# Part of a weight split moved from VectorE to GpSimd, and the matmul order around a triangular solve rewritten, in a hybrid decoder layer

## The chip, the cores and the metric

The kernel runs on one core of a Trainium2 chip. The metric is the device time of one execution in microseconds (us). The kernel before took 1213.77 us, the median of three runs (1211.12 to 1214.0). Engines are named as the profile names them: PE is TensorE, PEld its weight loads, DVE is VectorE, ACT is ScalarE, POOL is GpSimd and SP is SyncE, which here only issues loads.

## The reference, cut to what matters

One layer of a decoder for 256 tokens of width 2048, in float32:

```python
h = rms_norm(x, attn_norm_g)
proj = h @ w_in                                  # 2048 -> 4448 columns
h_r, h_k, h_v, h_w, h_a, h_g = token_shift(...)  # RWKV-7 heads, 16 x 64
c_q, c_kv, k_pe = ...                            # latent attention, 512 + 512 + 64
y_rwkv = rwkv7_mixer(...)                        # a recurrence over the 256 tokens
y_mla = mla_mixer(...)                           # 8 heads, causal softmax over 256 keys
x = x + concat(y_rwkv, y_mla) @ w_out
x = x + conv_glu_ffn(rms_norm(x), ...)           # 2048 -> 2 x 5632 -> 2048
return rms_norm(x)
```

In the recurrence a state S of 64 by 64 per head is updated by `S = S*w + (S a) b + v k` for every token, and `S r` is read out. The result is compared in float32, so the matmuls can't simply be rounded to a shorter type.

## The kernel before, in words

**Weight pieces.** All weights come in pieces of 128 x 1024 float32 (512 KB). `piece` (line 125) loads one on SP's queue into `raw` (three buffers), lets ACT write a rounded copy `hi` (line 133, three buffers), and lets DVE write the rest, `lo = raw - hi` (line 134, three buffers). An input product (`prod_c`, line 170) is then, for a piece, 16 matmuls with `hi` (line 175, high and low part of the activations) and 8 with `lo` (line 178). One tile of 128 output columns of `w_in` takes two pieces, h = 0 and h = 1.

**Order of the layer.** First the tiles of the decay, the keys (1 to 8), the receptances (9 to 16) and the values (17 to 24), in `in_tile` (line 201). Then the latent tiles 27 to 34 (`latent_tile`, line 801; x = 0 for the query latent, x = 1 for the key/value latent, four tiles each), the products from the latents (`up_b`, `up_v`), the chunks of the recurrence, the attention heads, the output projection, and from about 475 us on the feed-forward part, which the change doesn't touch.

**The factor.** The recurrence is done in four chunks of 64 tokens, and each chunk needs the inverse of a triangular matrix. `solve` (line 582) makes it: the masked products go to DRAM and back into `Lp` (POOL queue, line 580), DVE scales `Lp` (line 590) and does 31 steps of two operations each (lines 594 and 596), each on the result of the one before, then a reordered copy `tp` (line 598); POOL's queue writes it to DRAM (line 604), reads it back as `T11` (line 608) and does the same for `TT` (lines 606 and 613). On PE, `solve_r` (line 639) needs `T11`, `solve_t` needs `TT`, and all chunks come after.

**What sets the order.** PE's order around the chunks is written out by hand (`manual_schedule`, line 978). The work that doesn't belong to the recurrence is cut into 30 *units*, which the generator `all_units` (line 926) hands out: units 1 to 8 are the half tiles of the query latent, 9 to 16 those of the key/value latent, 17 to 20 the first products from the latents (unit 18 with `latent_rs(1)` and `rope_q`, unit 20 with the broadcast of `rrB1`), 21 to 30 the rest. `unit(11)` issues eleven of them before `chunk_a(0)` and `solve_r`; nine more stand one by one between the parts `chunk_a`, `chunk_b`, `chunk_c` of the chunks, three between the parts of the factor, and the rest between the heads (`step`). All other engines and queues are ordered by a planner, which fills each engine in time order from its own cost estimates, with what is ready and stands first in the program; the order so made is fixed, and each engine works it off in order.

**Buffers that the change touches.** `chunk_a` to `chunk_c`, the heads and `gn_out` share three PSUM buffers named `ch` (line 97), and the products share three named `mm`. In `chunk_c` the new state of both halves (`pS`, then DVE lines 734 to 737) came first, and then the outputs of both halves (`py`, copied by ACT, line 744). In the last part, `gn_out(0)` (transposes `pyT`, line 791) came before `step(7)`, the last head.

Of the kernel before, what the change touches and what calls it, by code (L numbers as in the profile page):

```python
# [9 lines left out]
F32 = mybir.dt.float32  # L10
# [4 lines left out]
ALU = mybir.AluOpType  # L15
# [3 lines left out]
T = 256  # L19
# [35 lines left out]
def hybrid_layer(ctx: ExitStack, tc: tile.TileContext, a: dict, out: bass.AP):  # L55
    nc = tc.nc
    V, S, PE = nc.vector, nc.scalar, nc.tensor
# [39 lines left out]
    def ch(n="ch"):  # L97
        return ps.tile([P, 512], F32, tag="ch", name=nm(n), bufs=NCH)
# [23 lines left out]
    nc.scalar.dma_start(vec, a["vec"])  # L122


    def piece(src, dst=None):
        raw = sb.tile([P, 1024], F32, tag="raw", name=nm("raw"), bufs=NRAW)
        last_w[0] = nc.sync.dma_start(raw, src).ins
        if dst is None:
            hi = sb.tile([P, 1024], F32R, tag="hi", name=nm("hi"), bufs=NHI)
            lo = sb.tile([P, 1024], F32R, tag="lo", name=nm("lo"), bufs=NLO)  # L130
        else:
            hi, lo = (dst.rearrange("p k t -> p (k t)")[:, q * 1024:(q + 1) * 1024] for q in range(2))
        S.copy(hi, raw)  # L133
        last_lo[0] = V.tensor_tensor(lo, raw, hi.bitcast(F32), ALU.subtract).ins  # L134
        return hi, lo

    def xsplit(g):
# [10 lines left out]
    last_w, last_lo, last_x, last_sh = [None], [None], [None], [None]  # L148
# [21 lines left out]
    def prod_c(acc, pieces, act, kt0, n, first, last):  # L170
        hi, lo = pieces
        acc = acc[:, :T]
        for j in range(n):
            for s in range(2):
                PE.matmul(acc, hi[:, j * P:(j + 1) * P], act(kt0 + j)[:, s, :], start=first and j == 0 and s == 0,  # L175
                          stop=False, skip_group_check=True)
        for j in range(n):
            PE.matmul(acc, lo[:, j * P:(j + 1) * P], act(kt0 + j)[:, 0, :], start=False,  # L178
                      stop=last and j == n - 1, skip_group_check=True)
# [19 lines left out]
    x_hl = lambda k: xs_[k // 4][:, k % 4, :, :]  # L199

    def in_tile(i, pf=mm):
        acc = pf()
        for h in range(2):
            prod_c(acc, piece(a["win"][i, h]), x_hl, h * 8, 8, h == 0, h == 1)
        flush()
        return acc

# [196 lines left out]
    PC = con([P, 8, 4], "PC")  # L404
# [280 lines left out]
    def pairs(dst, hf, terms, first=True):  # L685
        for n, term in enumerate(terms):
            for a_ in range(4):
                p = hf * 4 + a_
                for h in range(2):
                    lhsT, rhs = term(p, a_, h)  # L690
                    PE.matmul(dst[HS[h], a_ * 64:(a_ + 1) * 64], lhsT, rhs,
                              start=first and n == 0 and a_ == 0, stop=True, skip_group_check=True)
# [28 lines left out]


    def chunk_c(c):
        for hf in range(2):
            if c < 3:
                pS = ch("pS")
                pairs(pS, hf, [lambda p, a_, h: (BKt[c][:, p, HS[h]], UV[c][:, p, HS[h]])])
                for h in range(2):
                    hs = HS[h]
                    sv = ST[hf][hs, :, hs]  # L730
                    pSv = pS[hs, 0:256].rearrange("p (a v) -> p a v", a=4)
                    pcb = PC[hs, hf * 4:hf * 4 + 4, c:c + 1].broadcast_to([64, 4, 64])
                    if c > 0:
                        V.tensor_tensor(sv, pSv, sv, ALU.add)
                        V.tensor_tensor(sv, sv, pcb, ALU.mult)
                    else:
                        V.tensor_tensor(sv, pSv, pcb, ALU.mult)
        for hf in range(2):
            if c == 0:
                py[hf] = ch("py")  # L740
            pairs(py[hf], hf, [lambda p, a_, h: (G1[c][hf][:, h * 4 + a_, 64:128], UV[c][:, p, HS[h]])], c == 0)
            for h in range(2):
                yv = yt[c // 2][HS[c % 2], hf * 512:(hf + 1) * 512].rearrange("p (a h v) -> p a h v", a=4, h=2)
                ylast[c] = S.copy(yv[:, :, h, :], py[hf][HS[h], 0:256].rearrange("p (a v) -> p a v", a=4)).ins

    def gn_vec(w):
        y = yt[w]
# [53 lines left out]
    def latent_tile(x, j, gname):  # L801
        if j == 0:
            cl.append([s4(F32R, "cl").rearrange("p (k s t) -> p k s t", k=2, s=2) for _ in range(2)])
            css[x] = t2("css")
        i, acc = 27 + x * 4 + j, mm()
        prod_c(acc, piece(a["win"][i, 0]), x_hl, 0, 8, True, False)
        yield
        prod_c(acc, piece(a["win"][i, 1]), x_hl, 8, 8, False, True)
        cr, ssum = t2("cr"), css[x]
        V.tensor_tensor(cr, acc[:, :T], rsB, ALU.mult)  # L810
        if j == 0:
            S.activation(ssum, cr, AF.Square)
        else:
            sq = t2("csq")
            S.activation(sq, cr, AF.Square)
            V.tensor_tensor(ssum, ssum, sq, ALU.add)
        h_, l_ = (cl[x][j // 2][:, j % 2, q, :] for q in range(2))
        S.activation(h_, cr, AF.Copy, scale=vv(gname, j))
        V.scalar_tensor_tensor(l_, cr, vv(gname, j), h_.bitcast(F32), ALU.mult, ALU.subtract)
        yield  # L820
# [23 lines left out]
    def up_b(src, i, x, dsts):  # L844
        pcs = piece(src[i])
        for j in range(2):
            acc = mm()
            prod_c(acc, (pcs[0][:, j * 512:(j + 1) * 512], pcs[1][:, j * 512:(j + 1) * 512]),
                   lambda k: cl[x][k // 2][:, k % 2, :, :], 0, 4, True, True)
            if x == 0:  # L850
                S.copy(dsts[j], acc[:, :T])
            else:
                V.tensor_tensor(dsts[j], acc[:, :T], rrB1, ALU.mult)

# [106 lines left out]
    def out_piece(half, c, i):  # L961
        if i == 0:
            oacc[c] = [mm(), ch() if (half, c) == (1, 1) else mm()]
        if half == 1 and i == 2:
            load_x1(c)
        prod_a(oacc[c], piece(a["wout"][half, c, i]), lambda k: y_hl(yhi, half, k),
               lambda k: y_hl(ylo, half, k), i * 2, 2, i == 0, i == 3)
        if i == 3:
            for tb in range(2):
                V.tensor_tensor(x1[c][:, tb, :], x1[c][:, tb, :], oacc[c][tb], ALU.add)  # L970
# [3 lines left out]
    def unit(n=1):  # L974
        for _ in range(n):
            next(units)

    with tc.manual_schedule(engines={mybir.EngineType.PE}):
        unit(11)
        chunk_a(0)  # L980
        solve_r()
        unit()
        solve_t()
        unit()
        chunk_b(0)
        unit()
        chunk_c(0)
        gn = gn_vec(0)
        for c in range(1, 4):
            unit()  # L990
            chunk_a(c)
            if c == 3:
                next(gn)
            unit()
            chunk_b(c)
            if c == 3:
                next(gn)
            unit()
            chunk_c(c)
        next(gn)  # L1000
        g2a = s4(n="g2a")
        g2b = s4(n="g2b")
        gnwb = [s4(n=n) for n in ("gnw", "gnb")]
        with tc.issue_after(ylast[1]):
            for t, n in zip(gnwb, ("gnw", "gnb")):
                nc.scalar.dma_start(t, a[n].broadcast_to([P, 1024]))
            nc.scalar.dma_start(g2a, a["g2"][0:P])
            nc.scalar.dma_start(g2b[64:96], a["g2"][P:160])
        def step(h):
            attend_t(h)  # L1010
            if h < 7:
                scores(h + 1)
            attend(h)
            next(gn, None)

        scores(0)
        unit()
        next(gn)
        unit()
        step(0)  # L1020
        unit()
        step(1)
        unit()
        step(2)
        unit()
        out_piece(1, 0, 0)
        step(3)
        unit(2)
        assert next(units, None) is None
        step(4)  # L1030
        next(gn)
        out_piece(1, 0, 1)
        step(5)
        assert next(gn, None) is None
        gn_gate(0)
        out_piece(1, 0, 2)
        step(6)
        out_piece(1, 1, 0)
        gn_out(0)
        step(7)  # L1040
        out_piece(1, 0, 3)
        for _ in gn_vec(1):
            pass
        for i in range(1, 4):
            out_piece(1, 1, i)
# [194 lines left out]
```

## Time and profile before

| what | before |
|---|---|
| median of three runs | 1213.77 us |
| the profiled execution: its time / its span | 1213.11 us / 1211.3 us |
| mean granted PE clock in it | 0.982 |
| PE busy in it | 1167.2 us, 96% |
| DVE, ACT, POOL busy in it | 818.0, 589.0, 65.4 us |
| products `lo` on DVE (line 134), count and mean | 376, 1225 ns |

All times of the profile count from the start of the span. A busy PE is a PE that has matmuls in its pipeline; where its granted clock falls, the same matmuls take longer and it is busy all the same. In the timeline, the bracket at the end of a row is the idle time of that engine before it and what ended it.

### The profile page before, as it was taken

How to read it: one execution, taken by the hardware profiler on the slowest of the kernel's cores; microseconds unless marked ns; L12 is line 12 of the kernel's file. 1: busy time of each engine (PE TensorE's matmuls, PEld its weight loads, DVE VectorE, ACT ScalarE, POOL GpSimd, SP SyncE). 2: the span in 40 equal slices, each digit the busy share in tenths (PEclk: the TensorE clock that was granted, in tenths of full speed). 3: DMA queues.
4: the chain of work that ended last, by engine and by line, in shares of the span. 5: the costliest groups of instructions: out<-in, count | busy, mean ns of one | idle time of the engine just before them, and what ended most of it. 6: DMA issues, size and time to landing. Idle time of an engine off the chain costs nothing.

```text
span 1211.3 us, 19591 instructions
## 1 busy us (share of the span) xinstructions
PE 1167.2 (96%) x7629; PEld 1029.9 (85%) x7629; DVE 818.0 (68%) x1339; ACT 589.0 (49%) x897; POOL 65.4 (5%) x192
## 2 busy tenths in 40 slices
PE   7999999699989999999999999999999999999996
PEld 7899999688876788888888888888888888888885
DVE  6798659748857666777777776444477777766563
ACT  6584346324444355555555554333455555554542
POOL 1600430110000001000000000000000000000000
PEclk9999999879999999999999999999999999999998
DMA  9544455523433455555555555555655555566662
GB/s 323 199 136 149 140 170 177 183 77 104 162 106 106 161 185 176 190 192 192 192 192 191 191 192 187 192 189 188 205 192 189 193 192 191 190 223 209 209 212 84
DMA packets 61485, 215.90 MB, mean 178 GB/s; under 512 B 7376, under 2 KB 8144, under 8 KB 61392
## 3 DMA queue, kind: packets, MB, share of 16 engines
q1 hardware_dynamic: 58544, 209.22, 52.4%
q0 software_dynamic: 2080, 3.38, 1.1%
q10 hardware_dynamic: 768, 2.05, 0.5%
q8 instruction: 60, 0.98, 0.3%
q14 instruction: 33, 0.27, 0.1%
HBM read 210.48 MB, written 3.41 MB: 177 GB/s over the span
## 4 chain that ended last, share of the span: by engine, by line
PE 68%; DVE 1%; issue 1%; ACT 0%; ACTq 0%
PE mm L163 27%; PE mm L166 13%; PE mm L195 9%; PE mm L196 9%; PE mm L197 9%; PE pxT L1068 0%; PE pgate L782 0%; PE pgate L783 0%; PE mm L175 0%; DVE lo L134 0%; PE po L920 0%; PE ch L196 0%; PE ch L195 0%; PE ch L197 0%; ACT pexp L898 0%
## 5 line engine op out<-in xcount | busy, mean ns | idle before, releaser
L134 DVE TENSOR_TENSOR lo<-raw,hi 128x1024 fp32r<-128x1024 f32 x376 | 460.4, 1225 | 293.3 <-ACT hi L133 284.3
L133 ACT CAST hi<-raw 128x1024 fp32r<-128x1024 f32 x376 | 395.1, 1051 | 503.3 <-PE mm L163 160.4
L163 PE MATMUL mm<-z,hi 128*128 128x512 f32 x1408 | 351.4, 392 | 0.0
L163 PEld LDWEIGHTS mm<-z,hi 128*128 128x128 f32 x1408 | 252.1, 188 | 43.4
L166 PEld LDWEIGHTS mm<-z,lo 128*128 128x128 f32 x1408 | 188.4, 188 | 14.3
L166 PE MATMUL mm<-z,lo 128*128 128x256 f32 x1408 | 191.6, 279 | 0.0
L175 PE MATMUL mm<-x,hi 128*128 128x256 f32 x1024 | 145.1, 292 | 9.9 <-ACT hi L133 8.0
L175 PEld LDWEIGHTS mm<-x,hi 128*128 128x128 f32 x1024 | 132.7, 196 | 12.5 <-ACT hi L133 8.0
L196 PE MATMUL mm<-lo,hh 128*128 128x512 f32 x336 | 130.9, 390 | 0.0
L197 PE MATMUL mm<-hi,hl 128*128 128x512 f32 x336 | 130.9, 390 | 0.0
L195 PE MATMUL mm<-hi,hh 128*128 128x512 f32 x336 | 119.8, 390 | 0.0
L178 PE MATMUL mm<-x,lo 128*128 128x256 f32 x512 | 76.5, 289 | 0.0
L197 PEld LDWEIGHTS mm<-hi,hl 128*128 128x128 f32 x336 | 63.1, 188 | 13.1
L195 PEld LDWEIGHTS mm<-hi,hh 128*128 128x128 f32 x336 | 63.1, 188 | 13.0
L196 PEld LDWEIGHTS mm<-lo,hh 128*128 128x128 f32 x336 | 63.1, 188 | 12.9
L178 PEld LDWEIGHTS mm<-x,lo 128*128 128x128 f32 x512 | 68.6, 196 | 0.6 <-issue 0.3
L196 PE MATMUL mm<-lo,yhi 128*128 128x512 f32 x120 | 48.1, 401 | 0.0
L197 PE MATMUL mm<-hi,ylo 128*128 128x512 f32 x120 | 47.8, 398 | 0.0
L195 PE MATMUL mm<-hi,yhi 128*128 128x512 f32 x120 | 47.5, 404 | 0.0
L1114 POOL MEMSET gt<- 128x2 f32 x44 | 4.3, 99 | 577.2 <-DVE hl L1126 573.4
L195 PEld LDWEIGHTS mm<-hi,yhi 128*128 128x128 f32 x120 | 23.0, 192 | 6.3 <-issue 1.5
L197 PEld LDWEIGHTS mm<-hi,ylo 128*128 128x128 f32 x120 | 23.0, 192 | 5.1
(291 smaller groups left out, 1111.6 us busy)
## 6 DMA issues: line engine op xcount, KB each, us to landing
raw<-in_wgu SPq DMA_DIRECT2D x176, 512.0 KB, 4.3
raw<-in_wdn SPq DMA_DIRECT2D x88, 512.0 KB, 4.3
raw<-in_win SPq DMA_DIRECT2D x70, 512.0 KB, 3.7
raw<-in_wout SPq DMA_DIRECT2D x32, 512.0 KB, 3.4
raw<-in_wuq SPq DMA_DIRECT2D x6, 512.0 KB, 3.3
xraw<-in_xT SPq DMA_DIRECT2D x4, 512.0 KB, 6.1
xt<-in_x SPq DMA_DIRECT2D x4, 512.0 KB, 6.8
raw<-in_wuk SPq DMA_DIRECT2D x4, 512.0 KB, 3.8
```

What stands on the lines that cost most here:

```text
L133: S.copy(hi, raw)
L134: last_lo[0] = V.tensor_tensor(lo, raw, hi.bitcast(F32), ALU.subtract).ins
L163: PE.matmul(acc, hi[:, j * P:(j + 1) * P], act(kt0 + j), start=first and j == 0, stop=False, skip_group_check=True)
L166: PE.matmul(acc[:, :T], lo[:, j * P:(j + 1) * P], act(kt0 + j)[:, 0, :], start=False, stop=last and j == n - 1, skip_group_check=True)
L175: PE.matmul(acc, hi[:, j * P:(j + 1) * P], act(kt0 + j)[:, s, :], start=first and j == 0 and s == 0, stop=False, skip_group_check=True)
L178: PE.matmul(acc, lo[:, j * P:(j + 1) * P], act(kt0 + j)[:, 0, :], start=False, stop=last and j == n - 1, skip_group_check=True)
L195: PE.matmul(accs[tb], ah, wh, start=first and j == 0, stop=False)
L196: PE.matmul(accs[tb], ah, wl, start=False, stop=False)
L197: PE.matmul(accs[tb], al, wh, start=False, stop=last and j == n - 1)
L1114: nc.gpsimd.memset(gt[:, 0:2], 0.0)
```

## The change

Five edits, all before 475 us of the span:

- The `lo` of every second piece (h = 1) of the value tiles 17 to 24 and of the four query latent tiles is written by POOL and not by DVE: 12 products. `last_lo` is then not set by them (it is only used further ahead, in the start).
- `unit(7)` in place of `unit(11)` ahead of `chunk_a(0)` and `solve_r`. The four units go elsewhere: one before `scores(0)`, one more after it, and one more after each of `step(1)` and `step(2)`; every unit in between comes four places later.
- `chunk_c` goes state of half 0, output of half 0, output of half 1, state of half 1.
- In `up_b` for the queries, the second of two copies out of PSUM is by DVE and not by ACT (6 copies).
- `step(7)` comes before `gn_out(0)`.

```diff
-    def piece(src, dst=None):
+    def piece(src, dst=None, eng=None):
...
-        last_lo[0] = V.tensor_tensor(lo, raw, hi.bitcast(F32), ALU.subtract).ins
+        sub = (eng or V).tensor_tensor(lo, raw, hi.bitcast(F32), ALU.subtract).ins
+        if eng is None:
+            last_lo[0] = sub
...
     def in_tile(i, pf=mm):
         for h in range(2):
-            prod_c(acc, piece(a["win"][i, h]), x_hl, h * 8, 8, h == 0, h == 1)
+            eng = nc.gpsimd if h and 17 <= i < 25 else None
+            prod_c(acc, piece(a["win"][i, h], eng=eng), x_hl, h * 8, 8, h == 0, h == 1)
...
     def chunk_c(c):
-        for hf in range(2):
-            if c < 3:
-                pS = ch("pS")
...
-        for hf in range(2):
+        def state(hf):
+            if c == 3:
+                return
+            pS = ch("pS")
...
+        def outp(hf):
             if c == 0:
                 py[hf] = ch("py")
...
+        state(0)
+        outp(0)
+        outp(1)
+        state(1)
...
     def latent_tile(x, j, gname):
-        prod_c(acc, piece(a["win"][i, 1]), x_hl, 8, 8, False, True)
+        prod_c(acc, piece(a["win"][i, 1], eng=nc.gpsimd if x == 0 else None), x_hl, 8, 8, False, True)
...
     def up_b(src, i, x, dsts):
             if x == 0:
-                S.copy(dsts[j], acc[:, :T])
+                (V.tensor_copy if j else S.copy)(dsts[j], acc[:, :T])
...
-        unit(11)
+        unit(7)
         chunk_a(0)
         solve_r()
...
+        unit()
         scores(0)
-        unit()
+        unit(2)
         next(gn)
         unit()
         step(0)
         unit()
         step(1)
-        unit()
+        unit(2)
         step(2)
-        unit()
+        unit(2)
         out_piece(1, 0, 0)
         step(3)
         unit(2)
...
         out_piece(1, 1, 0)
+        step(7)
         gn_out(0)
-        step(7)
         out_piece(1, 0, 3)
```

More of the change, by code (lines that the diff above doesn't have):

```diff
@@ L723, in chunk_c @@
     def chunk_c(c):
-        for hf in range(2):
-            if c < 3:
-                pS = ch("pS")
[L727 to L737, printed above, removed]
-        for hf in range(2):
+        def state(hf):
+            if c == 3:
+                return
+            pS = ch("pS")
+            pairs(pS, hf, [lambda p, a_, h: (BKt[c][:, p, HS[h]], UV[c][:, p, HS[h]])])
+            for h in range(2):
+                hs = HS[h]
+                sv = ST[hf][hs, :, hs]
+                pSv = pS[hs, 0:256].rearrange("p (a v) -> p a v", a=4)
+                pcb = PC[hs, hf * 4:hf * 4 + 4, c:c + 1].broadcast_to([64, 4, 64])
+                if c > 0:
+                    V.tensor_tensor(sv, pSv, sv, ALU.add)
+                    V.tensor_tensor(sv, sv, pcb, ALU.mult)
+                else:
+                    V.tensor_tensor(sv, pSv, pcb, ALU.mult)
+        def outp(hf):
             if c == 0:
```

## The prediction, made before the result was known

> **What bounds the kernel now.** I read the page first, then the stretches of 10 us, then the timeline of each engine round the widest gap. The page says that PE is the engine to count:
>
> ```profile
> PE 1167.2 (96%) x7629; PEld 1029.9 (85%) x7629; DVE 818.0 (68%) x1339; ACT 589.0 (49%) x897; POOL 65.4 (5%) x192
> ```
>
> So only stretches where PE isn't busy or not at full clock can be won, and all edits lie between 140 and 400 us. By stretches (columns: busy time of PE, PEld, DVE, ACT, POOL, then PE's granted clock):
>
> ```profile
> 220.00:230.00 10.00, 10.00 (x87) 10.00 (x87) 9.13 (x19) 4.53 (x7) 0.00 (x0) 1.00 0.69 209
> 230.00:240.00 10.00, 2.83 (x47) 2.55 (x46) 7.39 (x31) 1.05 (x1) 1.55 (x3) 0.77 0.43 128
> 240.00:250.00 10.00, 5.94 (x138) 5.77 (x139) 2.76 (x4) 0.00 (x0) 4.72 (x6) 0.50 0.45 136
> 250.00:260.00 10.00, 10.00 (x156) 9.79 (x156) 2.92 (x4) 2.20 (x3) 0.00 (x0) 0.67 0.15 56
> ```
>
> PE is full until 230, stands, and then runs at half clock. PE's timeline names the wait, `solve_r` for T11:
>
> ```profile
> 222.65 2.05 PE L175 MATMUL mm<-x,hi 128*128 128x256 f32 x16
> ...
> 225.48 2.05 PE L175 MATMUL mm<-x,hi 128*128 128x256 f32 x16
> ...
> 231.67 1.15 PE L691 MATMUL px<-UV,G 128*64 128x64 f32 x32
> 243.48 0.28 PE L646 MATMUL pR<-T,G 32*32 32x32 f32 x2 [10.65 <-DMA T<-dU]
> 244.34 3.62 PE L646 MATMUL pR<-T,G 32*32 32x32 f32 x126 [0.58 <-DMA T<-dU]
> 247.89 3.78 PE L175 MATMUL mm<-x,hi 128*128 128x256 f32 x16
> ...
> 252.98 4.55 PE L661 MATMUL pT<-TT,RT 32*32 32x32 f32 x128
> 257.46 3.78 PE L175 MATMUL mm<-x,hi 128*128 128x256 f32 x16
> ...
> 262.83 1.15 PE L691 MATMUL px<-XB,TT 128*64 128x64 f32 x32
> ```
>
> A unit costs 225.48 - 222.65 = 2.83 us at full clock; the two behind the stall cost 5.09 and 5.37, together 4.8 us too much. T11 is late because DVE ends the 31 steps late. DVE's timeline, and its groups between 180.6 and 237.4:
>
> ```profile
> 180.62 1.22 DVE L590 TENSOR_TENSOR Lp<-Lp,Mp 128x1024 f32<-128x1024 f32 x1
> ...
> 236.39 1.04 DVE L598 COPY tp<-Tq 128x1024 f32<-128x1024 f32 x1
> ```
>
> ```profile
> 180.60:237.40 56.80, 52.37 (x122) 0.98 0.57 178
> ```
>
> ```profile
> L134 DVE TENSOR_TENSOR lo<-raw,hi 128x1024 fp32r<-128x1024 f32 x19 | 23.2, 1221 | 2.5 <-ACT hi L133 2.3
> L596 DVE TENSOR_TENSOR Tq<-Tq,tm 128x31 f32<-128x31 f32 (+15 forms) x31 | 10.5, 340 | 0.4
> L594 DVE TENSOR_TENSOR tm<-Tq,Lp 128x31 f32<-128x31 f32 (+15 forms) x31 | 10.5, 338 | 0.3
> L810 DVE TENSOR_TENSOR cr<-mm,rsB 128x256 f32<-128x256 f32 x5 | 2.1, 425 | 1.6 <-PE mm L178 1.6
> ```
>
> DVE is 92% busy there (52.37 of 56.80), the steps take 21.0 of it and 18 lo products that start there 22.0 (the 19th began before). From the end of `tp` (237.43) to T11 (244.34, DMA out and back) go 6.9 us.
>
> **The change part by part.** I reckon by when `solve_r` can start, then by what is left behind it.
>
> *T11 earlier.* Off DVE before the end of the steps: (a) of the 18 products, seven go to POOL (second pieces of tiles 22 to 24 and units 2, 4, 6, 8), 7 x 1.22 = 8.5 us. (b) Four units go behind the factor, with four products (4.9 us), two `cr` and one each of `css` and `cl`, about 1.7, and the root of `latent_rs(0)`, twelve short operations that I put at 2.3. Together 8.9. DVE then ends at 237.4 - 17.4 and T11 is there at 226.9, if POOL's products cost DVE nothing. PE is at `solve_r` four units sooner, 231.67 + 1.15 - 4 x 2.83 = 221.5, and waits 5.4 us instead of 11.2.
>
> *What a POOL product costs.* The trace has none of this size. From below: a POOL memset of the same size, which reads nothing. From above: three such passes, two reads and a write, 2.9 us. I take 2.4. Whether PE sees it: it needs `lo` when its `hi` matmuls are done.
>
> ```profile
> 168.61 0.97 POOL L586 MEMSET Tq<- 128x1024 f32 x1
> ```
>
> ```profile
> 213.43 1.05 ACT L133 CAST hi<-raw 128x1024 fp32r<-128x1024 f32 x1 [0.55 <-PE mm L175]
> ```
>
> ```profile
> 218.88 1.10 PE L178 MATMUL mm<-x,lo 128*128 128x256 f32 x8
> ```
>
> This `hi`, done at 214.48, is used from 217.00 and its `lo` from 218.88, so there are 4.4 us; a wait of one DVE operation (1.2) and 2.4 to 2.9 fit. The POOL queue can spoil that: a product of tile 18 falls among the 16 DMA issues for dL (157.08 to 165.72, next fence). Queued behind them it comes up to 5 us late for PE; ahead of them, `Lp` comes 2.4 us late, though it could have been scaled from 172.6 (168.06, 0.56 to issue and 4.0 to land). Both vanish in the wait for T11, so I price them at nothing; without that cover up to 5 us.
>
> ```profile
> 157.08 8.64 POOL L551 DMA_DIRECT2D dL<-G  x16 [14.66 <-DVE G L543]
> ...
> 168.06 0.56 POOL L580 DMA_DIRECT2D Lp<-dL  x1 [2.23 <-DMA dL<-G]
> ```
>
> The open cost is what a POOL product does to DVE. Around 33 us small POOL copies meet `lo` products:
>
> ```profile
> 32.45 1.19 POOL L302 COPY sinR<-rp 32x64 f32<-32x64 f32 x1
> 33.71 1.41 POOL L304 TENSOR_SCALAR sinR<-rp 32x64 f32<-32x64 f32 x1
> ...
> 40.24 0.23 POOL L302 COPY sinR<-rp 32x64 f32<-32x64 f32 x1
> 40.54 0.36 POOL L304 TENSOR_SCALAR sinR<-rp 32x64 f32<-32x64 f32 x1
> ```
>
> ```profile
> L134 DVE TENSOR_TENSOR lo<-raw,hi x376: 1212/1226/1245, 7.9 to 1184.5; 128x1024 fp32r<-128x1024 f32 x188
> ```
>
> The POOL copy takes 0.23 us alone and 1.19 beside a product: POOL waits for DVE. The other way the trace shows nothing; no product of 376 took over 1.245. So the price per POOL product on DVE lies between 0 and its full 2.4. I take 0, the end that rows show, and keep the other as a rival. The Trainium skill, SBUF — State Buffer, "SBUF: two separate sides", speaks against this: GpSimd and a DVE operation with two SBUF inputs share a port pair, the first holds it for the whole instruction and the other fully blocks. The POOL rows agree; by that rule DVE would be held too, which is the rival below.
>
> *PE behind the factor.* `solve_r` starts 244.3 - 226.9 = 17.4 us sooner, four units of 2.83 are still to do: +11.3. The slow clock costs 4.8 now; after a wait half as long, between 4.8 and 0, I take half: -2.4. In sum -8.5.
>
> *Order in `chunk_c`.* Three waits lie there, as the three `ch` buffers run out:
>
> ```profile
> 269.37 0.69 PE L691 MATMUL py<-UV,G 128*64 128x64 f32 x16 [0.81 <-DVE ST L737]
> ...
> 284.87 0.69 PE L691 MATMUL pS<-UV,BKt 128*64 128x64 f32 x16 [1.07 <-DVE ST L734]
> ...
> 304.04 1.12 PE L691 MATMUL pS<-UV,BKt 128*64 128x64 f32 x16 [2.83 <-DVE ST L734]
> ```
>
> They sum to 4.7; the last also slows the clock (1.12 for 16 matmuls against 0.69). Two outputs between the two states give DVE 1.1 to 1.4 us, and a unit still lies between the second state and the next chunk. I take -4 (0 to -5).
>
> *Later units.* Four piece loads move back on SP's queue with their units, where DMA is idle half of the time: nothing. But `rope_q` is now in unit 18, inside chunk 3. From ACT's copy to the last rotation went:
>
> ```profile
> 290.51 0.37 ACT L851 COPY qr<-mm 128x256 f32<-128x256 f32 x1
> ```
>
> ```profile
> 301.24 1.22 DVE L860 TENSOR_TENSOR qr<-qr,qs 128x1024 f32<-128x1024 f32 x1
> ```
>
> 11.6 us, four POOL DMAs and three DVE operations in it. Between unit 18 and `scores(0)` PE now has `chunk_b(3)`, two units from the latents and `chunk_c(3)`, which I put at 7.5 (1.15 for each chunk part, as for `px` above, and 2.6 for a unit with its small extras). So a new wait of up to 4 us; I take +2.5, for DVE has less queued. The six copies that go from ACT to DVE are of equal length: nothing, at most 6 x 0.4 us if DVE is last.
>
> *`step(7)` first.* It takes these waits and the clock behind them:
>
> ```profile
> 386.86 0.55 PE L913 MATMUL ptp<-cst,pexp 128*128 128x128 f32 x3 [2.13 <-DVE ylo L795]
> 388.03 0.70 PE L920 MATMUL po<-pT,vm 128*128 128x256 f32 x2 [0.62 <-ACT pT L914]
> ...
> 389.45 0.63 PE L197 MATMUL mm<-hi,ylo 128*128 128x512 f32 x1
> ```
>
> ```profile
> L196 PE MATMUL mm<-lo,yhi 128*128 128x512 f32 x120 | 48.1, 401 | 0.0
> ```
>
> 2.75 us, and about nine matmuls at 0.63 against a mean of 0.40, about 2. Some wait for a `ch` buffer comes back (1 to 1.5): -3 (0 to -4.5).
>
> **Sum**: -8.5 - 4 + 2.5 - 3 = -13. Against the profiled execution's own time (1213.1, with 1.8 us outside the span) that is 1200.1; it lay 0.7 under the median shown, so I say 1201.
>
> **Rivals.**
>
> *DVE is held by POOL.* Place: DVE between 180 and 240. Price: each of the seven products holds DVE for its own length. T11 then comes at 226.9 + 7 x 2.4 = 243.7, when PE has done four units less: the wait grows to 22 us and the sum turns to 1201 + 16.8 = 1218, slower. The slow clock is not saved either, but if DVE's fixed order also holds back PE's own products, PE arrives later and the wait is no longer than now; the two offset within 3 us. It decides against the change from a hold of about 13 / 7 = 1.9 us on. For it: POOL really waits for DVE in the rows above, and most of DVE's operations in this stretch have two SBUF inputs. Against: no product was ever stretched. In the Trainium skill, GPSIMD Engine Reference, "Elementwise — side-by-side cycle accounting", 2048 elements take 4497 ns on GpSimd; half of it is 2.25, an estimate by which this rival would end at 1217.
>
> *The solve starts earlier too.* `Lp` had landed by 172.6 and waited for its place until 180.62, with DVE half idle. If the planner puts it forward, T11 is there when PE comes at 221.5: the wait of 5.4 goes, and the rest of the slow clock: 1201 - 5.4 - 2.4 = 1193.
>
> *The later parts take it back.* The edits round T11 do what they say, but the new wait before `scores(0)` is 4 us with a slow clock behind it (another 2), `chunk_c` and `gn_out` only shift their waits (+7 of what I took): 1201 + 3.5 + 7 = 1211, no change that can be told.
>
> **How the numbers follow.** Forecast (1195 to 1207) 0.44; held DVE (1210 to 1222) 0.27; early solve (1190 to 1196) 0.11; taken back (1207 to 1214) 0.18. Of the forecast and the early solve nearly all is faster by over 0.3% (3.6 us, about what a measurement of this kernel tells from no change), of the part taken back a third, of held DVE a tenth: 0.63 faster. Held DVE gives 0.16 of slower, the late parts and a POOL queue that holds PE 0.05 more: 0.21; the rest, 0.16, is no change. Both signs are in play, so the range runs from 1194 to 1218; the forecast's own is 1195 to 1207.
>
> **What would show it.** Right: DVE's `lo`, 594 and 596 keep their durations while POOL runs its products; `tp` ends near 220, T11 lands near 227, PE waits 4 to 7 us in `solve_r`; no wait over 1 us in `chunk_c`; 2 to 4 us before `scores(0)`. Wrong: rows of 594 and 596 at 2 us and more beside a POOL product, `tp` past 230; or L178 waiting for POOL's `lo`.

## The result, and the profile after

The changed kernel takes 1227.05 us (median of seven runs, 1219.75 to 1229.25) against 1213.77 for the kernel before on the same chip: a ratio of 1.0107 with a 95% interval of 1.0075 to 1.0140. It is slower by 13 us, where I had forecast 1201 and a gain. Its profiled execution is the fastest of the seven, 1219.75 with a span of 1218.0, so the profile shows half of the loss: span against span (1218.0 against 1211.3) it is 6.7 us. The other half goes with the clock. The profiled execution had a mean granted clock of 0.985, the median run 0.979, and 0.006 of 1218 us is 7.3 us. Of the runs below, one of e1_all_dve (4033.85 us) and one of e16_thirteen (1698.34) fell in a slow state and are left out of every median and ratio.

Everything that differs lies ahead of the feed-forward part, as was expected: its first matmul starts at 475.39 before and at 482.03 after, and the span grows by about as much. By stretches (columns as in the prediction: PE, PEld, DVE, ACT, POOL, granted clock, DMA share, GB/s), the kernel after:

```profile
160.00:170.00 10.00, 8.17 (x71) 7.97 (x69) 6.31 (x3) 4.44 (x9) 7.95 (x9) 1.00 0.24 65
190.00:200.00 10.00, 7.17 (x38) 7.20 (x39) 8.12 (x20) 3.72 (x7) 4.08 (x6) 0.66 0.62 209
...
230.00:240.00 10.00, 0.00 (x0) 0.00 (x0) 9.58 (x24) 1.75 (x3) 0.00 (x0) 0.65 0.48 158
240.00:250.00 10.00, 0.27 (x2) 0.18 (x2) 3.10 (x10) 0.00 (x0) 4.70 (x7) 0.50 0.35 105
```

and one row of the kernel before for the first of them:

```profile
160.00:170.00 10.00, 10.00 (x87) 9.88 (x86) 5.16 (x7) 4.27 (x8) 7.55 (x17) 1.00 0.48 136
```

Two losses are to be seen. PE is no longer full ahead of the factor: between 160 and 170 it has gaps, and the transfers fall from 136 to 65 GB/s. And the stall in `solve_r` is twice as wide. PE's timeline of the kernel after names the waits:

```profile
168.31 0.44 PE L634 MATMUL pv<-cst,sh 128*128 128x128 f32 x2 [1.83 <-DVE sh L391]
178.57 3.10 PE L177 MATMUL mm<-x,hi 128*128 128x256 f32 x24 [0.99 <-ACT hi L133]
192.83 3.76 PE L177 MATMUL mm<-x,hi 128*128 128x256 f32 x16 [4.35 <-DVE Tq L599]
249.74 0.28 PE L649 MATMUL pR<-T,G 32*32 32x32 f32 x2 [20.67 <-DMA T<-dU]
250.46 3.62 PE L649 MATMUL pR<-T,G 32*32 32x32 f32 x126 [0.45 <-DMA T<-dU]
```

T11 is used at 250.5 instead of 244.3 although four units fewer stand ahead of it. POOL's timeline (start, length, then the operation, and in brackets what it waited for) shows the queue that the products joined:

```profile
154.48 7.62 POOL L554 DMA_DIRECT2D dL<-G  x14 [3.37 <-DVE G L546]
162.10 2.42 POOL L134 TENSOR_TENSOR lo<-raw,hi 128x1024 fp32r<-128x1024 f32 x1
164.44 1.10 POOL L554 DMA_DIRECT2D dL<-G  x2
...
165.59 2.37 POOL L134 TENSOR_TENSOR lo<-raw,hi 128x1024 fp32r<-128x1024 f32 x1
178.59 2.42 POOL L134 TENSOR_TENSOR lo<-raw,hi 128x1024 fp32r<-128x1024 f32 x1 [10.63 <-ACT hi L133]
180.95 0.58 POOL L583 DMA_DIRECT2D Lp<-dL  x1
```

The products of tiles 19, 20 and 21 run at 162.1, 165.6 and 178.6. The first stands behind 14 DMA issues, the third waits 10.6 us for its cast, and the load of `Lp`, issued at 168.06 before, goes out behind it at 180.95. DVE's timeline of the same kernel shows what runs beside these products:

```profile
162.28 3.33 DVE L134 TENSOR_TENSOR lo<-raw,hi 128x1024 fp32r<-128x1024 f32 x1
165.54 2.72 DVE L391 SCALAR_TENSOR_TENSOR sh<-h,vec,sh 128x256 f32<-128x256 f32 x1
...
188.89 1.22 DVE L593 TENSOR_TENSOR Lp<-Lp,Mp 128x1024 f32<-128x1024 f32 x1
...
205.33 2.46 DVE L599 TENSOR_TENSOR Tq<-Tq,tm 128x192 f32<-128x192 f32 x1
207.82 0.37 DVE L597 TENSOR_TENSOR tm<-Tq,Lp 128x207 f32<-128x207 f32 x1
```

A low part of 1.22 us takes 3.33, a shift of 0.48 takes 2.72, a step of 0.36 takes 2.46, and the step after it 0.37 again: each of the three ends within one normal length of the end of a product on POOL (164.52, 167.96 and, beside the step, 207.58). `Lp` is scaled at 188.89 instead of 180.62. Over the whole stretch the steps' groups read, with the products' own group last:

```profile
L597 DVE TENSOR_TENSOR tm<-Tq,Lp 128x31 f32<-128x31 f32 (+15 forms) x31 | 16.9, 545 | 0.9
L599 DVE TENSOR_TENSOR Tq<-Tq,tm 128x31 f32<-128x31 f32 (+15 forms) x31 | 14.7, 476 | 0.8
...
L134 POOL TENSOR_TENSOR lo<-raw,hi 128x1024 fp32r<-128x1024 f32 x12 | 30.0, 2503 | 49.7 <-ACT hi L133 44.3 <-PE mm L180 5.2 <-issue 0.2
```

The steps take 31.6 us instead of 21.0. So the rival "DVE is held by POOL" came about as it was described, and something else beside it, ahead of the solve, that I had priced at nothing.

### The profile page after: what moved, and what is told of

The parts are those of the page before. It is cut to its first block, busy times and chain, and to the rows that moved or that the text cites. A ratio compares the mean times of both kernels' runs of the same rounds, so it can differ in the third digit from the quotient of the medians.

```text
span 1218.0 us, 19594 instructions
## 1 busy us (share of the span) xinstructions
PE 1160.7 (95%) x7629; PEld 1022.4 (84%) x7629; DVE 823.4 (68%) x1333; ACT 587.0 (48%) x891; POOL 95.6 (8%) x204
## 4 chain that ended last, share of the span: by engine, by line
PE 69%; DVE 0%; ACT 0%; issue 0%; ACTq 0%
PE mm L165 26%; PE mm L168 13%; PE mm L197 9%; PE mm L198 9%; PE mm L199 9%; PE pgate L793 0%; PE pgate L792 0%; PE mm L177 0%; PE pxT L1079 0%; PE psc L900 0%; PE psc L898 0%; PE ch L199 0%; PE ch L197 0%; PE ch L198 0%; PE pyT L801 0%; PE mm L180 0%
## 5 line engine op out<-in xcount | busy, mean ns | idle before, releaser
L134 DVE TENSOR_TENSOR lo<-raw,hi 128x1024 fp32r<-128x1024 f32 x364 | 448.8, 1233 | 284.9 <-ACT hi L133 281.4
L134 POOL TENSOR_TENSOR lo<-raw,hi 128x1024 fp32r<-128x1024 f32 x12 | 30.0, 2503 | 49.7 <-ACT hi L133 44.3
```

Of the source, the lines that this page charges most:

```text
L134: sub = (eng or V).tensor_tensor(lo, raw, hi.bitcast(F32), ALU.subtract).ins
```

## The experiments

Three theories stood at the start. **Hold**: each product on POOL holds DVE for its length. **Queue**: the products ahead of the solve stand in POOL's order among DMA issues and spoil the loads and `Lp`. **Units**: seven units ahead of the factor are too few, whatever POOL does. Ratios are against the kernel before on the same chip; 0.1% is 1.2 us.

| run | products on POOL | units ahead | ratio | 95% |
|---|---|---|---|---|
| after | 17 to 24, four latents | 7 | 1.0107 | 1.0075 to 1.0140 |
| e1_all_dve | none | 7 | 1.0006 | 0.9987 to 1.0025 |
| e2_pool_only | as after, nothing else changed | 11 | 1.0104 | 1.0075 to 1.0133 |
| e3_rear_only | none, rear edits alone | 11 | 0.9979 | 0.9961 to 0.9997 |
| e4_late_pool | 22 to 24, four latents | 7 | 1.0022 | 1.0004 to 1.0040 |
| e5_two_more | 17, 18 and e4's | 7 | 1.0022 | 1.0008 to 1.0036 |
| e6_only19 | 19 | 7 | 0.9998 | 0.9982 to 1.0015 |
| e15_only20 | 20 | 7 | 0.9985 | 0.9969 to 1.0000 |
| e14_19_20 | 19, 20 | 7 | 1.0045 | 1.0026 to 1.0064 |
| e10_front3 | 19, 20, 21 | 7 | 1.0116 | 1.0090 to 1.0142 |
| e9_no21 | as after without 21 | 7 | 1.0092 | 1.0067 to 1.0117 |
| e13_free7 | e4's seven left out | 7 | 0.9935 | 0.9909 to 0.9962 |

### The parts of the change

```diff
 e1_all_dve, against the changed kernel
-            eng = nc.gpsimd if h and 17 <= i < 25 else None
+            eng = None
-        prod_c(acc, piece(a["win"][i, 1], eng=nc.gpsimd if x == 0 else None), x_hl, 8, 8, False, True)
+        prod_c(acc, piece(a["win"][i, 1]), x_hl, 8, 8, False, True)
 e2_pool_only: the kernel before with these lines and piece() of the changed kernel
 e3_rear_only: the kernel before with chunk_c, step(7) and the copies of the changed kernel
```

> The changed kernel with every low part on DVE again; seven units ahead of the factor and the new order of chunk_c and of the outputs stay. If the POOL products are the cause (they hold DVE, or stand before the load of Lp), the steps go back to 0.34 us each, tp ends near 228 (237.4 less 8.9 us of moved unit work) and T11 is in use near 235; PE is there at about 222 and waits 13 us, and the time is 1211 to 1215, some 13 below the changed kernel. If the smaller number of units is the cause, T11 comes no earlier than in the changed kernel (about 249) and the time stays near 1227.

> The kernel before with nothing but the twelve products given to POOL; eleven units stay ahead of the factor. By the theory of the hold and of POOL's queue together, Lp is scaled 8 us later and the steps take 30 us instead of 21, less 8.5 us of products that DVE no longer has: T11 8 to 14 us later, time 1223 to 1232. If the POOL products were free, as I forecast, T11 is 8.5 us earlier and the time falls to 1203 to 1208.

> The kernel before with only the order in chunk_c, step(7) ahead of gn_out and the copies to DVE; eleven units, all low parts on DVE. If these edits gain what I forecast (4 and 3 us), the time is 1205 to 1209 with solve_r where it was (244). If they only shift their waits, 1212 to 1215.

Without POOL's products the changed kernel is where the kernel before is (1212.90 against 1212.99), and the products alone cost as much as the whole change (1222.92, a ratio of 1.0104 against 1.0107). So POOL's part is the loss, and the theory of the units falls: `solve_r` starts at 238.8 in e1_all_dve, 11 us before the changed kernel, with the steps at 21.05 us. The rear edits alone gain 0.21%, 2.5 us, where I had counted 7. The move of the four units is what lies between e3_rear_only and e1_all_dve: it shows no gain (0.9979 and 1.0006, intervals that overlap).

### The hold beside the steps

```diff
 e4_late_pool, against the changed kernel
-            eng = nc.gpsimd if h and 17 <= i < 25 else None
+            eng = nc.gpsimd if h and 22 <= i < 25 else None
 e13_free7, against e4_late_pool: the seven products are not made
         S.copy(hi, raw)
+        if eng is not None:
+            return hi, hi
 e7_kinds, against the kernel before, behind the scaling of Lp
+        s_ = con([P, 448], "s_")
+        G.tensor_copy(s_, Lp.rearrange("p i t -> p (i t)")[:, 0:448])
+        for _ in range(4): G.memset(s_, 0.0)
+        for _ in range(4): G.tensor_copy(s_, s_)
+        for _ in range(4): G.tensor_scalar(s_, s_, 1.0, None, ALU.mult)
+        for _ in range(4): G.tensor_tensor(s_, s_, s_, ALU.mult)
```

> The changed kernel with POOL products only for tiles 22 to 24 and the four latents, the seven that run beside the steps; the five ahead of them are on DVE, and in POOL's order all seven stand behind the load of Lp. If POOL's queue costs as much as the hold, Lp is scaled near 180.6 again and T11 comes 8 us earlier than in the changed kernel (241 to 243), while the steps still take 30 us and more: time 1214 to 1219. If the hold alone is the cause and the late load was covered by it, T11 stays near 249 and the time near 1227.

> The kernel of e4_late_pool with the seven products beside the steps left out: their second pass of matmuls takes hi again in place of lo, so these values are wrong in their low parts while PE's work is the same. That is the price of nothing that my forecast took. If the sum ahead of solve_r was right for that price, the steps take 21 us, T11 comes 8.5 us sooner than in e1_all_dve (about 230 by its clock) and PE waits 5 to 9 us: time 1203 to 1206. If DVE's fixed order or the slow clock gives the gain back, 1208 to 1213.

> The kernel before with idle work on POOL from the scaling of Lp on: one copy out of Lp, then on a scratch tile of 128x448 four memsets, four copies, four tensor_scalars and four tensor_tensors, one after the other. Nothing else changes. If only an operation of POOL that reads two SBUF tensors holds DVE, the steps beside memset, copy and tensor_scalar keep 0.2 to 0.43 us, and those beside the four tensor_tensors (about 1.1 us each) take 1 us and more. If any POOL operation that reads SBUF does, the steps beside the copies are long too; if any that touches it, those beside the memsets as well. If POOL waits instead, POOL's rows grow and the steps stay.

In e4_late_pool all seven products run beside the steps, and the first of the steps' two groups alone has doubled, from 10.5 to 21.3 us; both take 34.1:

```profile
L597 DVE TENSOR_TENSOR tm<-Tq,Lp 128x31 f32<-128x31 f32 (+15 forms) x31 | 21.3, 688 | 0.8
```

Yet it is only 0.16% (2 us) slower than e1_all_dve, a difference that the intervals don't tell from none. The 13 us of holding are set against 8.5 us of products that DVE no longer makes, and `Lp` comes sooner (177.3 against 182.3, of which 2.0 us is a later start of e1's profiled execution), since one low part fewer stands ahead of it on DVE. When the same seven products are left out (e13_free7), 0.71% (8.6 us) is won over e1_all_dve and 0.87% (10.5 us) over e4_late_pool. PE is at `solve_r` when I had forecast for the change, but waits 10.2 us there and not 5.4:

```profile
219.77 1.15 PE L696 MATMUL px<-UV,G 128*64 128x64 f32 x32
230.84 0.28 PE L651 MATMUL pR<-T,G 32*32 32x32 f32 x2 [9.92 <-DMA T<-dU]
```

The hold therefore eats what the move was to bring, and by these ratios some 2 us more. It is not the loss of 13 us.

What holds DVE is told by e7_kinds. DVE's timeline, beside four memsets (182.4 to 184.4), four copies (184.5 to 187.9), four tensor_scalars (188.0 to 193.9) and four tensor_tensors (193.9 to 198.2) of POOL:

```profile
183.74 0.18 DVE L607 TENSOR_TENSOR Tq<-Tq,tm 128x31 f32<-128x31 f32 x1
...
185.17 0.58 DVE L607 TENSOR_TENSOR Tq<-Tq,tm 128x60 f32<-128x60 f32 x1
...
189.07 0.27 DVE L607 TENSOR_TENSOR Tq<-Tq,tm 128x112 f32<-128x112 f32 x1
...
195.42 0.98 DVE L607 TENSOR_TENSOR Tq<-Tq,tm 128x175 f32<-128x175 f32 x1
```

and POOL's own rows:

```profile
184.49 1.20 POOL L597 COPY s__2203<-s__2203 128x448 f32<-128x448 f32 x2
185.75 2.19 POOL L597 COPY s__2203<-s__2203 128x448 f32<-128x448 f32 x2
188.04 1.38 POOL L599 TENSOR_SCALAR s__2203<-s__2203 128x448 f32<-128x448 f32 x1
193.94 4.29 POOL L601 TENSOR_TENSOR s__2203<-s__2203 128x448 f32<-128x448 f32 x4
```

Beside a memset a step keeps its 0.18. Beside a copy it takes 0.58 instead of 0.22, the copy's length; and where the copy came second, beside a low part, the copy was the one that waited (two of them take 2.19 instead of 1.20). Beside a tensor_tensor of about 1 us it takes 0.98 instead of 0.33. Beside a tensor_scalar of 1.38 us whole steps of 0.27 lie inside POOL's row, behind one that took 0.60 instead of 0.24: by these rows, whose lengths on POOL the profile gives as rough, it holds DVE for a part of its time only. As the Trainium skill puts it, SBUF — State Buffer, "SBUF: two separate sides", a DVE instruction with two SBUF inputs contends with a GpSimd instruction that reads SBUF and not with one that only writes it, and whoever comes first keeps the shared port pair for the whole instruction. Memset, copy and tensor_tensor agree with it here; the rows beside tensor_scalar don't show the whole instruction.

### The products ahead of the solve

```diff
 the tiles whose second piece goes to POOL
 e5_two_more   against e4_late_pool:  + 17, 18
 e6_only19     against e1_all_dve:    + 19
 e15_only20    against e1_all_dve:    + 20
 e14_19_20     against e1_all_dve:    + 19, 20
 e10_front3    against e1_all_dve:    + 19, 20, 21
 e9_no21       against the changed kernel:  - 21
```

> The kernel of e4_late_pool with the products of tiles 17 and 18 on POOL as well; those of 19, 20 and 21 stay on DVE. 17 and 18 run before the 16 DMA issues for dL, beside DVE operations that read PSUM. If the loss of the changed kernel comes from the products that stand among the DMA issues and in front of the load of Lp (19 to 21), this one is like e4_late_pool: 1213 to 1217. If every product ahead of the solve costs its share of the 12.4 us between e4_late_pool and the changed kernel, it is 5 us slower: 1218 to 1221.

> The kernel of e1_all_dve with one single product on POOL, the second piece of tile 19, the one that stands behind 15 of the 16 DMA issues for dL. Theory of the queue: it runs at about 163 instead of 156, gives its load buffer back 7 us late, two loads of 512 KB start late, PE stands 2 to 4 us ahead of px and the two casts to hi after them are late; the solve starts as in e1_all_dve because nothing but this product is ahead of Lp: time 1215 to 1218, 2 to 5 over e1_all_dve, for one product. Theory of the hold alone: one product costs DVE at most 2.4 us away from the steps and is lost in the wait for T11: 1211 to 1214, as e1_all_dve.

> The changed kernel with the single product of tile 21 back on DVE; the other eleven stay on POOL. In POOL's order the load of Lp then has no product in front of it that waits for a late cast; those of 19 and 20 still stand round the last DMA issues for dL. If the load of Lp behind the product of 21 is what costs the changed kernel 12.4 us over e4_late_pool, Lp is issued near 168, scaled 8 us sooner than in the changed kernel, and the time is that of e5_two_more: 1213 to 1217. If the loss is spread over all five products ahead of the solve, a fifth of it goes: 1222 to 1226.

> The kernel of e1_all_dve with three products on POOL, those of tiles 19, 20 and 21; none runs beside the steps, so no step is held. If the order in POOL's queue alone makes the loss, Lp is issued near 181, T11 comes some 6 to 9 us later than in e1_all_dve, and the time is 1219 to 1224 although only three of twelve products are on POOL. If the held steps are needed for the loss, it stays at 1211 to 1215.

> The kernel of e1_all_dve with two products on POOL, those of tiles 19 and 20. Theory: the product of 19 waits behind 14 DMA issues, that of 20 follows at once, the two give their load buffers back late one after the other, the loads of 512 KB stand from 154 to 173 but for one, and the casts, DVE's low parts and Lp come late with them: time 1219 to 1225, as with three or twelve. If all three (19 to 21) are needed, 1211 to 1215.

> The kernel of e1_all_dve with one product on POOL, that of tile 20. It isn't queued behind DMA issues (they are out by 165.7) and needs no wait for another product; it only holds a DVE operation for 2.4 us. By the theory of the pair it costs nothing, 1211 to 1215, as 19 alone did; if the second product by itself makes the loss (it holds back sh and with it pv on PE), 1218 to 1224.

The products of 17 and 18 cost nothing (1.0022 with and without), and neither does 19 alone, against what I expected of it, nor 20 alone. The pair costs 0.39% over e1_all_dve (1217.07, between the two times that I had expected), and the three cost 1.10%, 13 us, as much as the whole change, with no product beside the steps. POOL's timeline of e10_front3:

```profile
162.82 2.41 POOL L134 TENSOR_TENSOR lo<-raw,hi 128x1024 fp32r<-128x1024 f32 x1
...
166.32 2.37 POOL L134 TENSOR_TENSOR lo<-raw,hi 128x1024 fp32r<-128x1024 f32 x1
179.26 2.42 POOL L134 TENSOR_TENSOR lo<-raw,hi 128x1024 fp32r<-128x1024 f32 x1 [10.57 <-ACT hi L133]
181.62 0.58 POOL L583 DMA_DIRECT2D Lp<-dL  x1
```

and the scaling of `Lp` on its DVE:

```profile
192.21 1.22 DVE L593 TENSOR_TENSOR Lp<-Lp,Mp 128x1024 f32<-128x1024 f32 x1
```

My first reading, that the load of `Lp` behind the product of 21 was the cause, fell with e9_no21. There `Lp` is issued at 171.0, and the time stays at 1222.8. DVE's timeline of e9_no21 says why:

```profile
189.54 2.24 DVE L134 TENSOR_TENSOR lo<-raw,hi 128x1024 fp32r<-128x1024 f32 x1 [4.39 <-ACT hi L133]
191.70 3.36 DVE L593 TENSOR_TENSOR Lp<-Lp,Mp 128x1024 f32<-128x1024 f32 x1
```

`Lp` has its place on DVE behind low parts whose casts are late, and those are late whether `Lp` has landed or not. The order of events is the same in the kernel after, e14_19_20, e10_front3 and e9_no21: two products in a row come late or hold DVE, a load buffer (there are three) is free late, the transfers thin out between 160 and 170 (29 to 71 GB/s in these four, against 115 to 136 in e1, e15 and before), the casts behind them wait for data, PE stands 4 to 8 us ahead of `px` (the last matmuls before `solve_r`), and DVE, which works in a fixed order, comes late to `Lp`. The waits of the load queue from 150 to 195 (total, times, longest) in the kernel before and after, and one of the casts in the kernel after:

```profile
SPq L127 <- DVE lo L134: 25.3, 8, 6.5
```

```profile
SPq L127 <- DVE lo L134: 20.9, 4, 10.9
SPq L127 <- DMA raw<-in_win: 11.2, 4, 3.6
```

```profile
177.47 1.04 ACT L133 CAST hi<-raw 128x1024 fp32r<-128x1024 f32 x1 [5.40 <-DMA raw<-in_win]
```

| run | start | Lp issued | Lp scaled | tp done | PE idle, 65 us to px |
|---|---|---|---|---|---|
| e15_only20 | 102.9 | 168.8 | 180.4 | 230.6 | 0.0 |
| e1_all_dve | 105.9 | 169.8 | 182.3 | 232.6 | 0.0 |
| e6_only19 | 102.1 | 168.0 | 183.5 | 231.1 | 0.6 |
| e14_19_20 | 102.2 | 168.6 | 188.1 | 236.7 | 3.8 |
| after | 101.6 | 181.0 | 188.9 | 243.4 | 7.2 |
| e9_no21 | 104.8 | 171.0 | 191.7 | 245.0 | 7.9 |
| e10_front3 | 102.3 | 181.6 | 192.2 | 242.0 | 8.0 |

("start" is when the matmuls `pg` of the factor begin, line 541 of the changed kernel, ahead of any product on POOL; the executions came to it up to 4.3 us apart, and this is to be taken off.) Counted from there, `tp` is done about 1.0 us later than in e1_all_dve in e15, 2.3 in e6, 7.8 in e14, 13.0 in e10, 13.5 in e9 and 15.1 in the kernel after, which is roughly the order of the losses.

That the pair and the three make the loss is shown. That the load buffers carry it is read from the traces; a fourth buffer, which would test it, wasn't tried. Thin transfers alone are not enough: e6_only19 has 78 GB/s between 160 and 170 and a load that waits 12.2 us for its buffer, scales `Lp` 5 us late from its start, and loses no time that can be told. Nor is POOL's queue told apart from the hold here. In the pair, the product of 20 holds the shift `sh` (2.75 instead of 0.48 us) and PE waits 1.85 us for it; in e15_only20 DVE is idle beside the product of 20 (165.2 to 169.3), so the run says nothing of that hold. The parts don't add up either: 21 costs 0.71% on top of the pair in e10_front3, and taking it out of the changed kernel brings no more than 0.15%, within the intervals.

### A faster version

```diff
 e8_dense, against e3_rear_only
-            if pp == 1 and g == 0:
+            if pp == 0 and g == 0:
                 solve()
-        with tc.issue_after(last_sh[0]):
             V.tensor_tensor(Lp, Lp, Mp.unsqueeze(1).broadcast_to([P, 32, 32]), ALU.mult)
 e11_no_copies, against e8_dense
-                (V.tensor_copy if j else S.copy)(dsts[j], acc[:, :T])
+                S.copy(dsts[j], acc[:, :T])
 e12_twelve, against e11_no_copies:  unit(11) -> unit(12), the last unit(2) -> unit()
 e16_thirteen, against e12_twelve:   unit(12) -> unit(13), the unit() behind step(2) left out
```

> The kernel of e3_rear_only with the solve put two tiles earlier in program order and not tied behind the last shift, so that Lp is scaled some three low parts sooner and the steps stand closer together in DVE's order; all low parts on DVE, eleven units. If DVE's place for Lp is what makes T11 late (it had landed by 172.6 and was scaled at 180.6), T11 comes 3 to 6 us earlier and the time falls by as much, to 1205 to 1208. If PE then waits for the low parts that the steps push back, it stays at 1210 to 1213.

> The kernel of e8_dense without the six copies moved from ACT to DVE (they go back to ACT); the rest of e8_dense stays. In e3_rear_only and e8_dense PE waits 2.0 us behind qn in up_b and 0.5 us at the diagonal behind it, which the kernel before does not. If the copies that moved to DVE make these waits, both go and the time is 1205.5 to 1207.5, 1 to 2.5 under e8_dense. If DVE is late there for another reason, it stays at 1208.

> The kernel of e11_no_copies with twelve units ahead of the factor and one less near the end of the units. e8_dense waits 2.4 us in solve_r with eleven, and PE runs at half clock from 238 to 260 although it hardly waits. If the wait is what slows the clock, a twelfth unit takes both away and the time falls by 2 to 6 us under e11_no_copies. If the clock falls with the small matmuls of solve_r and solve_t themselves, at most the 2.4 us of the wait are won, and T11 comes 1 to 2 us later for the unit's work on DVE: within 2 us of e11_no_copies.

> The kernel of e12_twelve with thirteen units ahead of the factor and one less behind step(2). In e12_twelve PE no longer waits for T11, so a thirteenth unit finds no wait to fill: 1201 to 1204 as e12_twelve if a unit costs the same at either place; under 1200 if units near the end of the attention cost more than ahead of the factor (e12_twelve won 6 us and only 2.7 of it was the wait); over 1205 if PE then lacks a unit at the waits behind scores.

| run | median us, before on its chip | ratio | 95% |
|---|---|---|---|
| e8_dense | 1208.35, 1212.20 | 0.9972 | 0.9959 to 0.9986 |
| e11_no_copies | 1208.10, 1211.87 | 0.9970 | 0.9955 to 0.9985 |
| e12_twelve | 1202.24, 1211.87 | 0.9911 | 0.9885 to 0.9936 |
| e16_thirteen | 1199.70, 1214.21 | 0.9908 | 0.9880 to 0.9936 |

With `Lp` put forward, T11 is used at 236.9 instead of 244.3 and the wait falls from 11.2 to 2.5 us; yet against e3_rear_only (0.9979) nothing is won that can be told. The copies are a miss: in e11_no_copies the wait of 2 us behind qn goes, waits of 0.4 and 1.0 stand elsewhere, and the time stays. A twelfth unit wins 7 us more, a thirteenth nothing that can be told. Both beat the kernel before by 0.9%, and so the changed kernel by some 2%. Where e8_dense lost its gain is in its stretches of 5 us:

```profile
245.00:250.00 5.00, 4.56 (x38) 4.34 (x39) 1.17 (x2) 1.04 (x1) 0.00 (x0) 0.50 0.02 3
250.00:255.00 5.00, 5.00 (x108) 5.00 (x106) 1.06 (x2) 0.58 (x1) 0.00 (x0) 0.50 0.35 108
255.00:260.00 5.00, 5.00 (x27) 4.94 (x26) 0.68 (x1) 1.59 (x2) 0.00 (x0) 0.50 0.00 0
```

PE runs at half clock up to 260 behind a wait of 2.5 us, and 3.3 us are lost already ahead of `px`, at 177, where it waits for DVE behind the scaling of `Lp` (which of DVE's operations it needed there isn't shown). In e16_thirteen, where the profile names no wait for T11, the same parts run at full clock in the profiled execution:

```profile
245.00:250.00 5.00, 3.75 (x63) 3.59 (x62) 4.38 (x9) 0.82 (x1) 0.00 (x0) 1.00 0.85 224
250.00:255.00 5.00, 4.62 (x133) 4.46 (x133) 2.29 (x3) 0.80 (x2) 0.00 (x0) 1.00 0.38 118
```

That execution is its fastest run (1196.60 at a mean clock of 0.993; the other four are at 0.986 to 0.991). In the profiled execution of e12_twelve the profile names no wait for T11 either, and PE has 0.50, 0.82 and 0.52 in the three stretches from 245 to 260. So the absence of the wait does not by itself bring the full clock.

## Why the prediction was wrong

**The step that failed first is the price of the products ahead of the solve, put at nothing under POOL's queue.** "Both vanish in the wait for T11, so I price them at nothing; without that cover up to 5 us." I had seen that a product would fall among the DMA issues for dL (I took it for tile 18's; it is tile 19's), and looked at what one late product costs PE or `Lp`. One product there does cost nothing that can be told (e6, e15). I didn't ask for several, nor follow them further. As the traces read, the product gives a load buffer back, the next 512 KB wait for the buffer, the next cast for the data, and DVE's fixed order puts `Lp` behind that cast. The wait for T11 is no cover for this, since the chain ends in T11: `tp` is done 13 us later. Three products ahead of the solve cost 13 us (e10 against e1) where the sum had 0; how much of it is the queue and how much the hold of DVE beside them stays open.

**The second is the price on DVE.** "I take 0, the end that rows show, and keep the other as a rival." The rows showed POOL waiting for DVE where DVE was first, and no case where POOL was. I took what wasn't seen for what isn't there. The product's own length was right (2.4 forecast, 2.50 measured), and in e4_late_pool the seven stretch the steps by 13.0 us, 1.9 each. The rival put the kernel at 1218; with the hold alone (e4) it is at 1.0022 of the kernel before, about 1216. There T11 is used at 240.2 and not at 243.7, since DVE makes one low part fewer ahead of `Lp` and scales it 3.3 us sooner than before. So the rival had the mechanism of this part, and the changed kernel, at 1227, is beyond it by the products ahead of the solve.

**With the price of nothing the sum ahead of the factor was three quarters right.** The seven free products were to bring T11 8.5 us sooner. In e13 against e1 it comes 8.1 us sooner, of which 1.9 is e1's later start; that the ratios differ by 8.6 us is in part luck. T11 was to be used at 226.9, 17.4 sooner than before, and is at 231.4. DVE ends `tp` at 224.5 and not at 220: from `Lp` to `tp` its busy time falls by 12.4 us (52.37 to 39.98) and not by 17.4, since one of the eleven products stood ahead of `Lp` and the rows of DVE overlap, so that their lengths add up to more than the time they take; it idles 7.1 us in its fixed order instead of 4.4; and `Lp` is scaled 3.1 us sooner. PE was to come at 221.5 and comes at 220.9. For the units alone the prediction's own terms promise little: T11 8.9 us sooner, and 11.3 us of units still to do.

**The slow clock.** "after a wait half as long, between 4.8 and 0, I take half: -2.4." No run bears this out: with a wait of 10 us (e13, `solve_r` from 230.8) the clock is back at 240, with one of 2.5 us (e8, from 235.8) only at 260.

**Behind the factor** the sizes were about right, in the profile. The kernel after:

```profile
271.78 0.69 PE L694 MATMUL pS<-UV,BKt 128*64 128x64 f32 x16 [0.96 <-DVE ST L741]
287.95 0.69 PE L694 MATMUL pS<-UV,BKt 128*64 128x64 f32 x16 [0.38 <-ACT yt L749]
303.92 0.69 PE L694 MATMUL pS<-UV,BKt 128*64 128x64 f32 x16 [0.65 <-ACT yt L749]
324.07 0.49 PE L898 MATMUL psc<-kn,qn 128*128 128x128 f32 x2 [1.03 <-DVE kn L863]
325.53 0.49 PE L900 MATMUL psc<-kpe,qr 128*128 128x128 f32 x2 [0.97 <-DVE qr L870]
...
393.83 0.70 PE L930 MATMUL po<-pT,vm 128*128 128x256 f32 x2 [0.97 <-ACT pT L924]
...
396.38 0.66 PE L801 MATMUL pyT<-cst,yt 128*128 128x128 f32 x4 [1.19 <-DVE ylo L933]
```

The three waits of `chunk_c` fell from 4.7 to 2.0 us and the last no longer slows the clock (-4 forecast). The new waits in `scores(0)` are 2.0 (2.5 forecast). Round step(7) waits of 2.75 became 0.97 + 1.19, and the matmuls at 0.63 run at 0.39 to 0.40: about 2.6 won of 3. From the use of T11 to the feed-forward part the kernel after takes 231.6 us against 231.1, with 11.3 us of units more; the terms had +4.4. Why e3_rear_only gains 2.5 us and not 7 stays open. Its PE has waits that the kernel before does not, 3.2 us in all between 296 and 317, the longest for qn:

```profile
300.59 1.21 PE L175 MATMUL mm<-cl,hi 128*128 128x256 f32 x8 [1.96 <-DVE qn L858]
```

This one follows a copy that moved to DVE, which I had put at nothing. But without the moved copies (e11) the wait is gone and the time is the same, so they are not shown to be the cause.

The range of 1194 to 1218 had the hold in its upper end and nothing for the products ahead of the solve, and so missed the time by 9 us. The bound of 5 us for it was taken from one product, and the bound for twelve wasn't asked.

## What to carry to other kernels

Before work is given to an engine that also issues transfers, list what its queue holds at that time and follow a late piece through the buffer it frees, to the next load and to the operation with a fixed place behind it: one late product was free here, two in a row cost 5 us and three 13. An elementwise product on GpSimd that reads SBUF is no free product while DVE works on two SBUF inputs; ask which DVE operations will run beside it, and count up to its whole length for each (here 1.9 of 2.5 us). When a trace shows a collision in one direction only, the other direction is unknown, and its price goes into the sum by both bounds.

## What the runs showed of the hardware that I had not expected

A POOL copy of 448 elements and a DVE step each wait for the other, whichever comes second: the step 0.58 instead of 0.22 us, two copies 2.19 instead of 1.20. Inside a tensor_scalar of 1.38 us two steps of 0.27 ran at their own length, as far as POOL's rough rows tell, and a memset doesn't touch them.

The stretch at half clock behind `solve_r` does not go with the length of the wait: from the first matmul of `solve_r` to the first state of `chunk_c` the same work takes 19.5 us after a wait of 21 us (after), 23.5 after 11 (before), 19.7 after 10 (e13), and 29.0 after 2.5 (e8). The Trainium skill, TensorE: Matmul & The Clock Gate, "What's actually happening", has full clock come back after one busy window of about 3.4 us. In e8_dense PE is busy 14.56 of the 15 us from 245 to 260 at a granted clock of 0.50, so here it took longer. What sets it, the sparse 32x32 matmuls or where the window falls, wasn't separated.

Runs of one kernel differ with this clock: the seven of the changed kernel go from 1219.75 at a mean clock of 0.985 to 1229.25 at 0.976, each slower one at a clock no higher. The loss of the profiled execution is told above row by row; why the others of this kernel had less clock wasn't profiled and stays open.
